# Seven products for eight in one pair of inner units of the FFN's down projection

## The chip, the cores and the metric

The program runs on one core of one Trainium2 chip, in one launch. The metric is the device time of one execution in microseconds (us), lower is better. It is compared as the median of several runs.

## The reference

One inference step of a two-layer streaming encoder for 512 prompt rows and 8 x 16 = 128 sample rows, 640 rows of width 1024 in all, which share the weights. Each layer is a mixer and a gated FFN, both between RMS norms:

```python
def swiglu(x, wg, wu, wd):
    return (jax.nn.silu(x @ wg) * (x @ wu)) @ wd
...
        xp = xp + rms_norm(mp, norm_mix_post[layer])
        fp = swiglu(rms_norm(xp, norm_ffn_pre[layer]), ffn_w_gate[layer], ffn_w_up[layer], ffn_w_down[layer])
        xp = xp + rms_norm(fp, norm_ffn_post[layer])
```

The hidden width is 2816, that is 22 units of 128. Everything is float32. Only the last product, `@ wd` (the down projection, 640 x 2816 by 2816 x 1024), is touched by the change.

## The kernel before

**Precision.** TensorE multiplies operands of type `fp32r`. To keep float32 accuracy each operand is split into a high part, a rounded copy made by ScalarE, and a low part, the rest, made by VectorE (`split`). A product then takes three matmuls: high by high, high by low and low by high.

**Rows.** The 640 rows are five row tiles of 128 (`TT = 5`), the last with the sample rows. For gate and up, the rows are cut into two halves of 320 (`HT`), and each hidden unit is made by the class `Seven`/`GateUp`: the two column blocks (gate and up), two inner halves and two row halves are a 2 x 2 x 2 block product, which is made with seven products for eight (the Winograd form of Strassen's scheme). Each product is 12 matmuls of 320 columns, so a unit takes 84 matmuls.

**Chunks.** `ffn` takes the 22 units in chunks of 4, 4, 4, 4 and 6 (`CHUNKS`). A chunk first makes its units' hidden rows, transposed, in tiles `hid` (128 inner rows by 640 columns, high and low part), and then runs `out_chunk`, the down stretch: for each row tile `t` and each column half `h` of 512, all units of the chunk are summed in one PSUM bank, with the hidden tile as the stationary operand and 512 columns of the unit's down weights as the moving one:

```python
            def products(h, i):
                for a, w in ((0, 0), (0, 1), (1, 0)):
                    mm(pss[h], acts[i][:, a, cols], weight(i, w, h), ...)
```

When the last unit is in, `leave(h)` takes the bank out: in the first chunk ScalarE copies it to the accumulator `acc[t]`, in later ones VectorE adds it there, with raised priority. So a chunk of four has 5 x 2 x 4 x 3 = 120 matmuls of 512 columns and ten reads of banks. In the first chunk of each FFN two units are made directly, without the seven products, before the other two (`Direct`, `PLAIN = 2`). The last chunk also ends the layer (`fin`), and isn't touched.

**Buffers.** Weights land in `raw` buffers (two, each for two units or for the gate and up of one), through SP's queue. `operand` splits them into `q` buffers (five); a gate-up unit takes four `q` (one of them for 512 columns only), a down stretch of four takes four. `hid` has seven buffers, `t2` (hidden work tiles) seven, PSUM eight banks, `t4` nine, five of which are the accumulator.

**Order.** The generators of all tasks are woven in Python by a clock of estimated matmul times (`Weave`); in the FFN's first four chunks the main task is alone but for the start of the first. The tile framework then sets the order of instructions on each engine before the program runs: an instruction goes into its engine's queue when it is ready by the framework's own estimate, and of several ready ones the first in priority, which is the order of the program unless `tc.high_priority()` raises it. On the chip each engine goes through its queue in that order, with semaphore waits.

In the trace every matmul but the transposes has line L170 (`mm`), and every ScalarE and VectorE instruction L102 (the wrapper `Ordered`). Lines L217 and L219 load down weights, L521 and L522 the weights of a gate-up unit. The names are `ps` for a bank, `q` for operands, `hid` for the hidden tiles, `x` for the normed input, `t` for work tiles and the accumulator.

Of the kernel before, what the change touches and what calls it, by code (L numbers as in the profile page):

```python
# [9 lines left out]
F32R = mybir.dt.float32r  # L10
AF = mybir.ActivationFunctionType
ALU = mybir.AluOpType
AX = mybir.AxisListType

P = 128
D = 1024
# [3 lines left out]
NT = NP + NS  # L20
TT = NT // P
# [3 lines left out]
HT = NT // 2  # L25
# [8 lines left out]
PLAIN = 2  # L34
# [6 lines left out]
CACHE = 5200.0  # L41
LAND = 2500.0
DIRECT = ((8, 12),)


class Event:
# [62 lines left out]
def trunk_kernel(  # L109
# [41 lines left out]
    nc = tc.nc  # L151
    act, dve = Ordered(tc, nc.scalar), Ordered(tc, nc.vector)
# [4 lines left out]
    qp = ctx.enter_context(tc.tile_pool(name="qp", bufs=5))  # L157
# [9 lines left out]
    def mm(out, lhsT, rhs, start, stop, n, share=1, more=False):  # L167
        fast = lhsT.dtype == F32R
        W.now += PASS * (max(n, 256) if fast else 4 * n / share) + 2
        nc.tensor.matmul(out, lhsT=lhsT, rhs=rhs, start=start, stop=stop, skip_group_check=more)  # L170
# [7 lines left out]
    def nm(s):  # L178
        uid[0] += 1
        return f"{s}{uid[0]}"  # L180

    def bank(shape=(P, 512)):
        return psp.tile(list(shape), F32, tag="ps", name=nm("ps"))

    def t4(shape):
        return t4p.tile(list(shape), F32, tag="t4", name=nm("t4_"))

    def t2(shape):
        return t2p.tile(list(shape), F32, tag="t2", name=nm("t2_"))
# [19 lines left out]
    def raw():  # L209
        return rawp.tile([P, 5, 512], F32, tag="raw", name=nm("raw"))  # L210

    def fetch(srcs):

        for i, src in enumerate(srcs):
            if i % 2 == 0:
                w = raw()[:, :4, :].rearrange("p (h a) c -> p h (a c)", h=2)
                nc.sync.dma_start(out=w[:, 0, :], in_=src)  # L217
                if i + 1 < len(srcs):
                    nc.sync.dma_start(out=w[:, 1, :], in_=srcs[i + 1])  # L219
            yield w[:, i % 2, :]  # L220

    def operand(src):
        n = src.shape[-1]
        q = qp.tile([P, 2, D], F32R, tag="q", name=nm("q"))
        split((q[:, 0, :n], q[:, 1, :n]), src)
        return q

    def unit(feed):
        return operand(next(feed))

    def split(dst, val):
        act.copy(out=dst[0], in_=val)
        dve.tensor_tensor(out=dst[1], in0=val, in1=dst[0].bitcast(F32), op=ALU.subtract)
# [6 lines left out]
    class Norm:  # L240


        def __init__(self):
            self.ms = None
# [16 lines left out]
    class Normed:  # L261
# [8 lines left out]
        def take(self, t, ps):  # L270
            c = slice(t * P, (t + 1) * P)
            for i in range(2):
                split((self.h[i][:, :, c], self.l[i][:, :, c]), ps[i])
            W.signal(self.ev[t], 1600)
# [161 lines left out]
    def hid_tile():  # L436
        return hidp.tile([P, 2, NT], F32R, tag="hid", name=nm("hid"))

    def out_chunk(acts, srcs, acc, first, last, fin, tail=None):
        feed = fetch(srcs)  # L440
        hls = [unit(feed) for _ in srcs[:5]]
        n = len(acts)
        spare = [[t2([P, 512]).bitcast(F32R) for _ in range(2)] for _ in range(2)] if n > 5 else None
        if spare:
            x = next(feed)
            for h in range(2):
                split(spare[h], x[:, h * 512 : (h + 1) * 512])

        def weight(i, w, h):
            if i < 5:  # L450
                return hls[i][:, w, h * 512 : (h + 1) * 512]
            return spare[h][w]

        for t in range(TT):
            cols = slice(t * P, (t + 1) * P)
            if tail is not None and t == TT - 1:
                yield from tail()
            pss = [bank(), bank()]
            if first:
                acc[t] = t4([P, D])  # L460

            def products(h, i):
                for a, w in ((0, 0), (0, 1), (1, 0)):
                    mm(
                        pss[h],
                        acts[i][:, a, cols],
                        weight(i, w, h),
                        i == 0 and a == 0 and w == 0,
                        i == n - 1 and a == 1,
                        512,  # L470
                    )

            def leave(h):
                o = acc[t][:, h * 512 : (h + 1) * 512]
                if first:
                    act.copy(out=o, in_=pss[h])
                else:
                    with tc.high_priority():
                        dve.tensor_tensor(out=o, in0=pss[h], in1=o, op=ALU.add)
                if last:  # L480
                    fin(t, h, acc[t], pss[h])

            early = n - 1 if t == 0 else EARLY if t == TT - 1 else 0
            for i in range(early):
                for h in range(2):
                    products(h, i)
                yield
            for h in range(2):
                for i in range(early, n):
                    products(h, i)  # L490
                    if i % 2 and i < n - 1:
                        yield
                leave(h)
                yield

    def in_row(t):
        return xp[t * P : (t + 1) * P, :] if t < 4 else xs

# [83 lines left out]
    class GateUp(Seven):  # L582


        def __init__(self, layer, f, X):
            super().__init__(wgate[layer, f], wup[layer, f], X)
            self.one = t2([P, 2, HT])
            self.two = t2([P, 2, HT])
            self.p5 = self.two[:, 1, :]
            self.hid = hid_tile()  # L590
# [12 lines left out]
        def c21(self, a):  # L603
            gate, up = self.two[:, 0, :], self.two[:, 1, :]
            act.activation(out=gate, in_=a, func=AF.Silu)
            dve.tensor_tensor(out=up, in0=up, in1=gate, op=ALU.mult)
            split((self.hid[:, 0, HT:], self.hid[:, 1, HT:]), up)

    class Units(Seven):

# [49 lines left out]
    class Direct(Plain):  # L660
# [4 lines left out]
        def leave(self, col, cols, ps):  # L665
            if col == 0:
                self.t = t2([P, 2, HT])
                act.activation(out=self.t[:, 0, :], in_=ps, func=AF.Silu)
            else:
                t = self.t[:, 1, :]  # L670
                dve.tensor_tensor(out=t, in0=ps, in1=self.t[:, 0, :], op=ALU.mult)
                split((self.hid[:, 0, cols], self.hid[:, 1, cols]), t)
# [16 lines left out]
    def ffn(layer, X, make):  # L689
        hid = {}  # L690
        acc = {}
        f0 = 0
        for c, n in enumerate(CHUNKS):
            fs = list(range(f0, f0 + n))
            rest = fs
            if c == 0:
                rest = fs[PLAIN:]
                lead = [Direct(layer, f, X) for f in fs[:PLAIN]]
                for low in range(2):
                    for i, g in enumerate(lead):  # L700
                        yield from g.rows(low)
                        if (low, i) == (0, PLAIN - 1):
                            ahead = GateUp(layer, rest[0], X)
                            ahead.prepare()
                for f, g in zip(fs, lead):
                    hid[f] = g.hid
            for f in rest:
                g = ahead if f == PLAIN else GateUp(layer, f, X)
                yield from g.steps()
                hid[f] = g.hid  # L710
            last = c == len(CHUNKS) - 1
            yield from out_chunk(
                [hid[f] for f in fs],
                [wdown[layer, f * P : (f + 1) * P, :] for f in fs],
                acc,
                c == 0,
                last,
                make() if last else None,
            )
            f0 += n  # L720
# [5 lines left out]
    def even_mixer(X, hls):  # L726
# [58 lines left out]
        def pairs(todo):  # L785
# [3 lines left out]
            def make():  # L789
                i, j, _ = todo[len(made)]  # L790
                p = (PlainUnits if (i, j) in DIRECT else Units)(ev_t[i], ev_t[j], X)
                p.prepare()
# [99 lines left out]
        def mixed_pair(g):  # L892
# [17 lines left out]
            False,  # L910
            True,
            make_fin(gpost, in_row, x_row, X2),
        )
        return X2
# [368 lines left out]
    def main():  # L1283
# [4 lines left out]
        def load(t):  # L1288
            xt.append(t4([P, D]))
            nc.sync.dma_start(out=xt[t], in_=in_row(t))  # L1290
# [52 lines left out]
        def mid():  # L1343
            gpost = bcast(g_ffn_post[0], D, t4)
            nxt.append(Normed(bcast(g_mix_pre[1], D, t4)))
            return make_fin(gpost, x_row, x_row, nxt[0])

        yield from ffn(0, X, mid)
        X = yield from odd_mixer(nxt[0])

        def end():
            gpost = bcast(g_ffn_post[1], D, t4)
            return make_fin(gpost, x_row, y_row, None)

        yield from ffn(1, X, end)

    W.spawn(main(), 9)
# [95 lines left out]
```

## Time and profile before

| what | value |
|---|---|
| median of 3 runs | 1312.57 us (1312.55 to 1312.61) |
| the profiled execution | 1312.65 us, of which the span is 1310.9 us |
| TensorE busy | 1293.6 us, 99% of the span |
| weight loads (PEld, beside the matmuls) | 1178.0 us, 90% |
| VectorE (DVE) busy | 891.6 us, 68% |
| ScalarE (ACT) busy | 615.3 us, 47% |
| granted TensorE clock | 0.999 of full speed |

A row of a timeline gives the start from the span's begin, the time up to the end of the group, engine, line, operation, what it writes and reads, the shapes, the count, and in brackets the idle time before it and what ended that. A row of the groups ends in the busy time in us, the mean of one instruction in ns, and the idle time before. A row of the stages gives, for a stretch from A to B, its length and the busy time of each engine with the number of instructions in brackets. Matmuls overlap, so the time of one is read from the distance of the starts, not from its mean duration.

### The profile page before, as it was taken

Reading aid. Unit: us, or ns where it says so; the run is one execution under the profiler, and the core shown is the slowest. Engines: PE = TensorE matmul, PEld = TensorE weight load, DVE = VectorE, ACT = ScalarE, POOL = GpSimd, SP = SyncE. Lnnn points to the kernel's source line nnn. Section 1 sums busy time; section 2 is a strip of 40 time slices with the busy share of each in tenths; the row PEclk is TensorE's granted clock in tenths of the full one; section 3 lists DMA queues with packets and bytes.
Section 4 is the critical chain, followed back from the end, with each engine's and each line's share of the span. In section 5 each row is a group of like instructions: output and inputs, shape, how many; then the busy total and the mean of one; then the engine's idle time right before and its main releaser. Section 6 shows DMA issues by size and latency. Waiting matters only on the chain. (4 is left out here: it accounts for less than half of the span.)

```text
span 1310.9 us, 20085 instructions
## 1 busy us (share of the span) xinstructions
PE 1293.6 (99%) x8066; PEld 1178.0 (90%) x8066; DVE 891.6 (68%) x1458; ACT 615.3 (47%) x1134; POOL 54.4 (4%) x107
## 2 busy tenths in 40 slices
PE   8999999999999999999999999999999999999997
PEld 6999988989899998998799886689999898999996
DVE  7986779737576665777646555689567575766765
ACT  6545547535254352554433455466455252534541
POOL 2100110000000000001110000010000000000000
PEclk9999999999999999999999999999999999999999
DMA  7112452211223121245335435732213031221242
GB/s 251 73 65 97 146 177 97 97 63 68 95 80 114 65 97 56 75 148 189 143 120 185 154 139 195 287 130 89 97 64 129 32 116 46 97 97 64 97 140 102
DMA packets 45965, 150.12 MB, mean 115 GB/s; under 512 B 6576, under 2 KB 8496, under 8 KB 45872
## 3 DMA queue, kind: packets, MB, share of 16 engines
q1 hardware_dynamic: 45872, 148.84, 31.3%
q8 instruction: 63, 1.03, 0.3%
q14 instruction: 30, 0.25, 0.1%
HBM read 133.57 MB, written 15.26 MB: 114 GB/s over the span
## 5 line engine op out<-in xcount | busy, mean ns | idle before, releaser
L170 PE MATMUL ps<-x,q 128*128 128x320 f32 (+2 forms) x4884 | 727.5, 310 | 3.0 <-DVE q L102 1.8
L170 PEld LDWEIGHTS ps<-x,q 128*128 128x128 f32 x4884 | 717.6, 188 | 8.0 <-issue 2.9
L170 PE MATMUL ps<-q,hid 128*128 128x512 f32 x1710 | 402.8, 392 | 0.0
L102 ACT CAST q<-raw 128x1024 fp32r<-128x1024 f32 (+1 forms) x276 | 267.4, 976 | 281.3 <-PE ps L170 230.2
L102 DVE TENSOR_TENSOR q<-raw,q 128x1024 fp32r<-128x1024 f32 (+1 forms) x276 | 310.6, 1128 | 129.8 <-ACT q L102 125.0
L170 PEld LDWEIGHTS ps<-q,hid 128*128 128x128 f32 x1710 | 318.2, 188 | 67.2 <-ACT t L102 1.0
L102 ACT COPY t<-ps 128x320 f32<-128x320 f32 (+2 forms) x304 | 135.6, 452 | 198.2 <-PE ps L170 170.0
L102 DVE TENSOR_TENSOR t<-ps,t 128x512 f32<-128x512 f32 (+2 forms) x164 | 100.5, 616 | 92.6 <-PE ps L170 92.4
L102 DVE TENSOR_TENSOR raw<-raw 128x512 f32<-128x512 f32 x141 | 122.0, 866 | 5.0 <-DMA raw<-in_dram 2.8
L102 DVE TENSOR_TENSOR t<-t,t 128x512 f32<-128x512 f32 (+4 forms) x107 | 58.2, 552 | 48.7 <-ACT t L102 46.3
L237 POOL TENSOR_TENSOR st<-st,mhalf 128x1 f32<-128x1 f32 x45 | 30.4, 677 | 992.4 <-DVE st L102 988.4
L102 DVE SCALAR_TENSOR_TENSOR t<-t,st,t 128x512 f32<-128x512 f32 (+1 forms) x61 | 54.2, 916 | 21.2 <-POOL st L237 19.6
L102 ACT ACTIVATE t<-t 128x320 f32<-128x320 f32 (+1 forms) x60 | 40.2, 669 | 42.1 <-issue 22.7
L102 ACT ACTIVATE ps<-t 128x512 f32<-128x512 f32 x40 | 24.1, 604 | 63.3 <-DVE t L102 63.2
L102 ACT CAST hid<-t 128x320 fp32r<-128x320 f32 (+1 forms) x96 | 46.3, 484 | 9.5 <-DVE t L102 7.6
L102 DVE TENSOR_TENSOR t<-t 128x320 f32<-128x320 f32 (+3 forms) x90 | 48.8, 543 | 1.8 <-ACT t L102 0.4
L102 DVE TENSOR_TENSOR hid<-t,hid 128x320 fp32r<-128x320 f32 (+1 forms) x96 | 49.0, 513 | 0.1
L170 PE MATMUL ps<-q,x 128*128 128x512 f32 x192 | 46.5, 395 | 2.3 <-DVE q L102 1.8
L170 PEld LDWEIGHTS ps<-q,x 128*128 128x128 f32 x192 | 35.5, 188 | 11.4 <-DVE q L102 2.9
L102 DVE TENSOR_TENSOR t<-t,ps 128x320 f32<-128x320 f32 x47 | 22.9, 488 | 32.8 <-PE ps L170 32.8
L174 PE MATMUL ps<-ident,t 128*128 128x128 f32 x288 | 40.9, 276 | 3.2 <-DVE t L102 1.9
L174 PEld LDWEIGHTS ps<-ident,t 128*128 128x128 f32 x288 | 32.8, 140 | 11.4 <-issue 6.0
(97 smaller groups left out, 550.3 us busy)
## 6 DMA issues: line engine op xcount, KB each, us to landing
raw<-in_dram SPq DMA_DIRECT2D x184, 512.0 KB, 4.1
x<-in_dram SPq DMA_DIRECT2D x24, 512.0 KB, 6.4
t<-in_dram SPq DMA_DIRECT2D x22, 512.0 KB, 5.5
xbuf<-t SPq DMA_DIRECT2D x15, 512.0 KB, 2.8
t<-xbuf SPq DMA_DIRECT2D x15, 512.0 KB, 3.9
out_dram<-t SPq DMA_DIRECT2D x15, 256.0 KB, 2.0
c<-in_dram SPq DMA_DIRECT2D x4, 512.0 KB, 4.3
fscr<-x SPq DMA_DIRECT2D x2, 768.0 KB, 3.3
```

The source lines that it names most:

```text
L102: ins = op(*args, **kw)
L170: nc.tensor.matmul(out, lhsT=lhsT, rhs=rhs, start=start, stop=stop, skip_group_check=more)
L174: nc.tensor.transpose(out=out, in_=in_, identity=ident)
L237: nc.gpsimd.tensor_tensor(out=r, in0=ms, in1=mhalf, op=ALU.pow)
```

## The change

In each of the first four chunks of each FFN, one pair of inner units is taken out of the plain sums of the down stretch: units 0 and 1 of the chunk, in the first chunk units 2 and 3 (`CROSSED`). For this pair the down product is a 2 x 2 x 2 block product again: the inner halves are the two units, the column halves the two of 512, and the row halves are row tiles 0 and 1 against row tiles 3 and 4 (`FAR = 3`). It is made with seven products for eight. Row tile 2 and the other two units stay as they were, as plain products, which go into the same banks where they can.

- `Sums` makes four combinations of the pair's hidden rows (256 columns each) on VectorE from the unsplit values, in the work tiles that the two units hold, and splits them into two more `hid` buffers.
- `Weights` holds the pair's weights in one `raw` buffer, splits the plain ones into two `q` (`take`), then makes four combinations in place, in two steps of two (`early`: T2 and T1, `late`: T3 and T4), each step splitting into one `q` more.
- `crossed_chunk` stands in the place of `out_chunk`. Partial sums that serve two outputs are read from a bank while its sum goes on: bank `a[t]` is added to the left half of row tile t, then with S2 T2 to the right half, then with S3 T3 to the right half of row tile t + 3, then with the second unit's T4 and the plain units to the left half of row tile t + 3. Bank `c[t]` takes S1 T1 to row tile t + 3 and then S4 and the plain units to row tile t, right half.
- The first unit of a pair splits its lower hidden rows only up to row 384, since row tiles 3 and 4 of it are used in the sums alone (`low`).

```diff
+CROSSED = {0: ((2, 3),), 1: ((0, 1),), 2: ((0, 1),), 3: ((0, 1),)}
+FAR = 3
+Q = 2 * P
...
+    class Sums:
+        def __init__(self, one, two, hold):
+            a11, a21 = one.one[:, 1, :Q], one.two[:, 1, HT - Q :]
+            a12, a22 = two.one[:, 1, :Q], two.two[:, 1, HT - Q :]
+            s1, s2, s3, s4 = (x[:, 0, :Q] for x in (two.two, two.one, one.one, one.two))
+            self.s = [hold[i // 2][:, :, i % 2 * Q : (i % 2 + 1) * Q] for i in range(4)]
+            for i, (out, x, y, op) in enumerate(
+                (
+                    (s1, a21, a22, ALU.add),
+                    (s2, s1, a11, ALU.subtract),
+                    (s3, a11, a21, ALU.subtract),
+                    (s4, a12, s2, ALU.subtract),
+                )
+            ):
+                dve.tensor_tensor(out=out, in0=x, in1=y, op=op)
+                split((self.s[i][:, 0, :], self.s[i][:, 1, :]), out)
+
+    class Weights:
+        def __init__(self, srcs):
+            self.w = w = raw()
+            for i in range(2):
+                nc.sync.dma_start(out=self.both(i), in_=srcs[i])
+            self.q = []
+        def take(self, i):
+            self.q.append(operand(self.both(i)))
...
+        def sub(self, out, x, y):
+            w = self.w
+            dve.tensor_tensor(out=w[:, out, :], in0=w[:, x, :], in1=w[:, y, :], op=ALU.subtract)
+        def halves(self, x):
+            q = qp.tile([P, 2, D], F32R, tag="q", name=nm("q"))
+            q4 = q.rearrange("p x (a c) -> p x a c", a=2)
+            split((q4[:, 0], q4[:, 1]), x)
...
+        def early(self):
+            self.sub(4, 1, 0)
+            self.sub(0, 3, 4)
+            self.t2, self.t1 = self.halves(self.w[:, 0:5:4, :])
+        def late(self):
+            self.sub(1, 3, 1)
+            self.sub(2, 2, 0)
+            self.t3, self.t4 = self.halves(self.w[:, 1:3, :])
+
+    def crossed_chunk(acts, pairs, sums, srcs, acc, first):
+        ws = [Weights([srcs[i] for i in p]) for p in pairs]
+        for w in ws:
+            for i in range(2):
+                w.take(i)
...
+        for i in rest:
+            hls[i] = unit(feed)
+        for w in ws:
+            w.early()
+        for w in ws:
+            w.late()
...
+        def leave(t, h, ps):
+            o = acc[t][:, h * 512 : (h + 1) * 512]
+            if first and (t, h) not in written:
+                written.add((t, h))
+                with tc.high_priority():
+                    act.copy(out=o, in_=ps)
+                return
+            with tc.high_priority():
+                dve.tensor_tensor(out=o, in0=ps, in1=o, op=ALU.add)
...
+        near = range(TT - FAR)
+        a = [bank() for _ in near]
+        for t in near:
+            products(a[t], [(act_rows(p[0], t), wt(p[0], 0)) for p, _, _ in every])
+            leave(t, 0, a[t])
+            yield
+        for t in near:
+            b = bank()
+            products(b, [(act_rows(p[1], t), wt(p[1], 0)) for p, _, _ in every] + plain(t, 0))
+            leave(t, 0, b)
+            yield
+        for t in range(TT - FAR, FAR):
+            for h in range(2):
+                b = bank()
+                products(b, plain(t, h, range(len(acts))))
+                leave(t, h, b)
+                yield
+        c = [bank() for _ in near]
+        for n, (p, w, s) in enumerate(every):
+            begin, end = n == 0, n == len(every) - 1
+            for t in near:
+                products(a[t], [(sum_rows(s, 1, t), w.t2)], False, end)
+                if end:
+                    leave(t, 1, a[t])
+            yield
+            for t in near:
+                products(c[t], [(sum_rows(s, 0, t), w.t1)], begin, end)
+                if end:
+                    leave(t + FAR, 1, c[t])
+            yield
+        for t in near:
+            products(c[t], [(sum_rows(s, 3, t), wt(p[1], 1)) for p, _, s in every] + plain(t, 1), False)
+            leave(t, 1, c[t])
+            yield
+        for t in near:
+            products(a[t], [(sum_rows(s, 2, t), w.t3) for _, w, s in every], False)
+            leave(t + FAR, 1, a[t])
+            yield
+        if rest:
+            for t in near:
+                b = bank()
+                products(b, plain(t + FAR, 1))
+                leave(t + FAR, 1, b)
+                yield
+        for t in near:
+            products(a[t], [(act_rows(p[1], t + FAR), w.t4) for p, w, _ in every] + plain(t + FAR, 0), False)
+            leave(t + FAR, 0, a[t])
+            yield
...
     class GateUp(Seven):
-            split((self.hid[:, 0, HT:], self.hid[:, 1, HT:]), up)
+            split((self.hid[:, 0, HT : self.low], self.hid[:, 1, HT : self.low]), up[:, : self.low - HT])
...
     def ffn(layer, X, make):
-                g = ahead if f == PLAIN else GateUp(layer, f, X)
+                g = ahead if f == PLAIN else GateUp(layer, f, X, P * FAR if f - f0 in summed else NT)
                 yield from g.steps()
                 hid[f] = g.hid
+                made[f - f0] = g
+                for m, p in enumerate(crossed):
+                    if p[1] == f - f0:
...
+                        sums.append(Sums(*(made[i] for i in p), hold))
             last = c == len(CHUNKS) - 1
+            if crossed:
+                yield from crossed_chunk(
...
+                f0 += n
+                continue
             yield from out_chunk(
```

More of the change, by code (lines that the diff above doesn't have):

```diff
@@ new lines, in trunk_kernel, with both @@
+    class Weights:
[6 more added lines that the diff above has]
+            self.q.append(operand(self.both(i)))
+        def both(self, i):
+            return self.w[:, 2 * i : 2 * i + 2, :].rearrange("p a c -> p (a c)")
+        def sub(self, out, x, y):
[5 more added lines that the diff above has]
+            split((q4[:, 0], q4[:, 1]), x)
+            return ([q[:, x, a * 512 : (a + 1) * 512] for x in range(2)] for a in range(2))
+        def early(self):
[6 more added lines that the diff above has]
+            self.t3, self.t4 = self.halves(self.w[:, 1:3, :])
@@ new lines, in crossed_chunk, with wt, act_rows, sum_rows @@
+    def crossed_chunk(acts, pairs, sums, srcs, acc, first):
[3 more added lines that the diff above has]
+                w.take(i)
+        hls = {i: q for p, w in zip(pairs, ws) for i, q in zip(p, w.q)}
+        rest = [i for i in range(len(acts)) if i not in hls]
+        feed = fetch([srcs[i] for i in rest])
+        for i in rest:
[4 more added lines that the diff above has]
+            w.late()
+        every = list(zip(pairs, ws, sums))
+        written = set()
+        def wt(i, h):
+            return [hls[i][:, x, h * 512 : (h + 1) * 512] for x in range(2)]
+        def act_rows(i, t):
+            return [acts[i][:, x, t * P : (t + 1) * P] for x in range(2)]
+        def sum_rows(s, i, t):
+            return [s.s[i][:, x, t * P : (t + 1) * P] for x in range(2)]
+        def products(ps, parts, start=True, stop=True):
+            last = 3 * len(parts) - 1
+            for n, (a, b) in enumerate(parts):
+                for i, (x, y) in enumerate(((0, 0), (0, 1), (1, 0))):
+                    mm(
+                        ps,
+                        a[x],
+                        b[y],
+                        start and n + i == 0,
+                        stop and 3 * n + i == last,
+                        512,
+                        more=not (start and stop),
+                    )
+        def plain(t, h, units=rest):
+            return [(act_rows(i, t), wt(i, h)) for i in units]
+        def leave(t, h, ps):
[7 more added lines that the diff above has]
+                dve.tensor_tensor(out=o, in0=ps, in1=o, op=ALU.add)
+        if first:
+            for t in range(TT):
+                acc[t] = t4([P, D])
+        near = range(TT - FAR)
[46 more added lines that the diff above has]
+            yield
@@ L582, in trunk_kernel, with __init__ @@
     class GateUp(Seven):
-        def __init__(self, layer, f, X):
+        def __init__(self, layer, f, X, low=NT):
             super().__init__(wgate[layer, f], wup[layer, f], X)
+            self.low = low
             self.one = t2([P, 2, HT])
@@ L702, in ffn @@
                         if (low, i) == (0, PLAIN - 1):
-                            ahead = GateUp(layer, rest[0], X)
+                            ahead = GateUp(layer, rest[0], X, P * FAR if CROSSED.get(c) else NT)
                             ahead.prepare()
@@ L706, in ffn @@
                     hid[f] = g.hid
+            crossed = CROSSED.get(c, ())
+            summed = [p[0] for p in crossed]
+            made, sums = {}, []
             for f in rest:
-                g = ahead if f == PLAIN else GateUp(layer, f, X)
+                g = ahead if f == PLAIN else GateUp(layer, f, X, P * FAR if f - f0 in summed else NT)
                 yield from g.steps()
                 hid[f] = g.hid
-            last = c == len(CHUNKS) - 1
+                made[f - f0] = g
+                for m, p in enumerate(crossed):
+                    if p[1] == f - f0:
+                        hold = [
+                            t4([P, 2, 2 * Q]).bitcast(F32R) if m else hid_tile()[:, :, : 2 * Q] for _ in range(2)
+                        ]
+                        sums.append(Sums(*(made[i] for i in p), hold))
+            last = c == len(CHUNKS) - 1
+            if crossed:
+                yield from crossed_chunk(
+                    [hid[f] for f in fs],
+                    crossed,
+                    sums,
+                    [wdown[layer, f * P : (f + 1) * P, :] for f in fs],
+                    acc,
+                    c == 0,
+                )
+                f0 += n
+                continue
             yield from out_chunk(
```

## The prediction

> **What bounds the kernel now.** I read the busy shares first, then TensorE's own timeline, then the busy times stage by stage, then the groups of instructions by shape, and last the places where TensorE waited.
>
> ```profile
> span 1310.9 us, 20085 instructions
> ## 1 busy us (share of the span) xinstructions
> PE 1293.6 (99%) x8066; PEld 1178.0 (90%) x8066; DVE 891.6 (68%) x1458; ACT 615.3 (47%) x1134; POOL 54.4 (4%) x107
> ...
> PEclk9999999999999999999999999999999999999999
> ```
>
> TensorE is busy for 1293.6 of 1310.9 us at the full clock, so 17.3 us of idle time is all that anything other than fewer or shorter matmuls could win. VectorE at 68% is the next. The span and what lies around it make 1312.65 us for the profiled execution, 0.08 us above the median of the runs shown (1312.57); I make the sum against 1312.65 and take 0.08 off.
>
> ```profile
> 288.77 49.44 PE L170 MATMUL ps<-x,q 128*128 128x320 f32 x336
> 338.04 27.39 PE L170 MATMUL ps<-q,hid 128*128 128x512 f32 x120
> 365.27 49.44 PE L170 MATMUL ps<-x,q 128*128 128x320 f32 x336
> ```
>
> This is the second chunk of the first FFN: four gate-up units, 336 matmuls, then the down stretch, 120 matmuls. No idle time stands between the rows, so starts tell the pitch: (365.27 - 338.04) / 120 = 226.9 ns for a matmul of 512 columns, and (338.04 - 288.77) / 336 = 146.6 ns for one of 320.
>
> ```profile
> core 0: us, PE busy (x) PEld busy (x) DVE busy (x) ACT busy (x) POOL busy (x), PEclk, DMA share, GB/s
> 42.00:73.00 31.00, 31.00 (x220) 30.88 (x220) 28.48 (x49) 16.18 (x26) 5.08 (x11) 1.00 0.28 104
> 261.50:288.80 27.30, 27.30 (x123) 22.60 (x122) 7.42 (x11) 9.28 (x16) 0.00 (x0) 1.00 0.11 39
> 288.80:338.00 49.20, 49.20 (x337) 49.20 (x336) 36.62 (x51) 28.09 (x47) 0.00 (x0) 1.00 0.30 107
> 338.00:365.30 27.30, 27.30 (x123) 22.60 (x122) 13.37 (x20) 3.98 (x7) 0.00 (x0) 1.00 0.10 39
> ```
>
> In the down stretch (338.00 to 365.30) VectorE works 13.37 of 27.3 us and ScalarE 3.98; in the gate-up stretch before it 36.62 and 28.09 of 49.2. TensorE alone sets the time there. The first row matters too: with VectorE busy for 28.48 of 31.0 us (92%) TensorE still lost nothing.
>
> **What the change removes.** In a down stretch each row tile and column half takes 4 units x 3 matmuls, 5 x 2 x 12 = 120. Counted from the new function: 6 (first unit of the pair, row tiles 0 and 1, left half), 18 (second unit and the two plain ones there), 24 (row tile 2, both halves, all four units), 6, 6, 18, 6 (the products with T2, T1, S4 and T3), 12 and 18 (the plain units and T4 on row tiles 3 and 4): 114. All have 512 columns and the same 128x128 stationary tile. So 6 x 226.9 ns = 1.361 us go from each of eight stretches (four in each of two FFNs): **10.9 us**. This count also excludes that the change removes no work.
>
> [...]
>
> **What the change adds off TensorE.** The rows for one instruction of each kind:
>
> ```profile
> L102 DVE TENSOR_TENSOR q<-raw,q 128x1024 fp32r<-128x1024 f32 x227 | 277.0, 1224 | 87.2 <-ACT q L102 82.4
> L102 ACT CAST q<-raw 128x1024 fp32r<-128x1024 f32 x227 | 236.9, 1052 | 107.1 <-PE ps L170 62.4 <-issue 17.7 <-DVE t L102 12.6
> L102 DVE TENSOR_TENSOR t<-ps,t 128x512 f32<-128x512 f32 x106 | 72.5, 689 | 86.7 <-PE ps L170 86.6
> L102 DVE TENSOR_TENSOR raw<-raw 128x512 f32<-128x512 f32 x94 | 64.7, 688 | 4.6 <-DMA raw<-in_dram 2.8
> L102 DVE TENSOR_TENSOR hid<-t,hid 128x320 fp32r<-128x320 f32 x88 | 42.7, 486 | 0.1
> L102 DVE TENSOR_TENSOR x<-t,x 128x256 fp32r<-128x256 f32 x12 | 4.4, 420 | 0.3 <-ACT x L102 0.3
> L102 ACT CAST x<-t 128x256 fp32r<-128x256 f32 x12 | 4.1, 400 | 0.0
> L102 DVE TENSOR_TENSOR t<-t,f 128x256 f32<-128x256 f32 x6 | 2.6, 428 | 0.0
> L102 DVE TENSOR_TENSOR hid<-x,hid 128x128 fp32r<-128x128 f32 x4 | 1.0, 283 | 0.0
> ```
>
> - Four activation sums of 256 columns and their splits: VectorE 4 x 0.43 + 4 x 0.42 = 3.4 us, ScalarE 4 x 0.40 = 1.6 us.
> - Four weight differences of 512 columns, 4 x 0.69 = 2.8 us, and two splits of 1024, 2 x 1.22 = 2.4 us on VectorE and 2 x 1.05 = 2.1 us on ScalarE.
> - Partial sums leave the banks 18 times instead of 10: 8 x 0.69 = 5.5 us more on VectorE (in the first chunk the ten first writes stay on ScalarE, as now).
> - The first unit's lower hidden split shrinks from 320 to 64 columns: 0.2 to 0.3 us less.
>
> Together 13.8 us more VectorE and 3.5 us more ScalarE in a chunk. VectorE's 13.37 us in the down stretch become about 13.4 + 10.4 = 23.8 of 25.9 us (92%), the same share as in the stretch at 42 to 73 us, where TensorE lost nothing. In chunks 2 to 4 the sums fall into the third gate-up unit: VectorE has 49.20 - 36.62 = 12.6 us free in four units, 3.1 in one, against 3.4; the fourth unit takes the rest, and the sums aren't wanted before 48 matmuls (10.9 us) into the down stretch. In the first chunk the pair is the last two units, so its sums stand at the start of the down stretch; there VectorE has only 7.42 us to do, and the sums, the first weight pair and the unit's own rest (3.4 + 2.6 + some 2 us, four operations near 0.49) fit the 10.9 us. I cost all this at nothing. Without that cover the price is the part that overhangs: up to 2 us a chunk if VectorE runs that far behind.
>
> **Buffers and loads.** The transfers stay two times two 512 KB on SP's queue; the pair's raw buffer is held until T3 and T4 are split.
>
> ```profile
> 314.22 0.33 SPq L217 DMA_DIRECT2D raw<-in_dram  x1
> ...
> 331.82 0.33 SPq L521 DMA_DIRECT2D raw<-in_dram  x1
> ...
> 339.14 0.33 SPq L521 DMA_DIRECT2D raw<-in_dram  x1
> ```
>
> ```profile
> 361.43 0.62 ACT L102 CAST q<-raw 128x512 fp32r<-128x512 f32 x1 [21.02 <-PE ps L170]
> ```
>
> ```profile
> raw<-in_dram SPq DMA_DIRECT2D x184, 512.0 KB, 4.1
> ```
>
> (SP's timeline, ScalarE's, and the page's list of transfers with the time to landing.) The first down weights are asked for at 314.2, now and after, and land 4.1 us later, some 20 us before the stretch. The next two units' weights are now asked for at 331.8 and 339.1. After the change the first goes out when the plain pair's buffer is split (about 339) and the second when T3/T4 are split. T3/T4 need the operand buffer of the pair's first unit, free after 48 matmuls at 338.04 + 10.9 = 348.9, so cast (1.05) and split (1.22) end near 351.5. The second load lands 4.1 us later, some 8 us before the new end of the stretch (338.04 + 114 x 0.2269 = 363.9), and its unit comes a unit later still. Nothing else in these stretches is queued behind it on SP. T3 itself is wanted after 78 matmuls, 6.8 us after its buffer is free, 4.5 us more than it needs. The next unit's operands, which now wait for a buffer until 361.43, get T1/T2's buffer after 60 matmuls (351.7) and the second unit's after 72 (354.4). All hidden; if VectorE lagged by more than 4.5 us, T3 would be late next.
>
> One need moves forward: in the first chunk the last unit's hidden rows are wanted after 6 matmuls instead of 18.
>
> ```profile
> 261.54 27.39 PE L170 MATMUL ps<-q,hid 128*128 128x512 f32 x120
> ```
>
> ```profile
> 261.51 0.46 ACT L102 CAST hid<-t 128x320 fp32r<-128x320 f32 x1 [0.43 <-DVE t L102]
> ```
>
> ```profile
> 262.53 0.49 DVE L102 TENSOR_TENSOR hid<-t,hid 128x320 fp32r<-128x320 f32 x1
> ```
>
> Their high part is done at 261.97 and wanted at 261.54 + 1.36 = 262.90, the low part at 263.02 and wanted two matmuls later, 263.35. It is covered, by 0.3 us; if the sums came in between, up to 1 us in two of the eight stretches would be lost.
>
> **The one wait that I price.** One bank is filled with T1 products (row tile 3), read by VectorE, and then added to again by S4 products (row tile 0), with only row tile 4's three T1 matmuls between: 3 x 226.9 = 0.68 us.
>
> ```profile
> 343.23 1.28 DVE L102 TENSOR_TENSOR t<-ps,t 128x512 f32<-128x512 f32 x2
> ...
> 349.15 0.69 DVE L102 TENSOR_TENSOR t<-ps,t 128x512 f32<-128x512 f32 x1 [2.03 <-PE ps L170]
> ```
>
> The fourth group of 12 ends at 338.04 + 48 x 0.2269 = 348.93; its read starts at 349.15, 0.22 us after, and lasts 0.69. So the bank is free 0.91 us after its last matmul, and TensorE is ready after 0.68: 0.23 us are lost, and a return signal for which no row stands alone. From below the wait is zero, if other matmuls are put there; from above it is 0.23 + 1.22 = 1.45 us, if a split of 1024 has just begun. The trace shows that the planner does put other work there:
>
> ```profile
> 221.33 1.92 PE L170 MATMUL ps<-a,q 128*128 128x320 f32 x12
> 223.09 0.31 PE L170 MATMUL ps<-x,q 128*128 128x320 f32 x1
> 223.24 0.60 PE L170 MATMUL ps<-a,q 128*128 128x320 f32 x3
> 225.07 1.88 PE L170 MATMUL ps<-x,q 128*128 128x320 f32 x11 [1.23 <-DVE x L102]
> ```
>
> After one matmul of the second half three of the next column were drawn forward, though too few: 1.23 us were lost. I take 0.3 us a stretch, near the unfilled turn with VectorE free, since 0.68 us per three matmuls against four reads at 0.64 us each (1.28 for two) leaves it just in step. 8 x 0.3 = 2.4 us.
>
> **Sum.** 1312.65 - 10.9 + 2.4 = 1304.2, less 0.08: **1304.1 us**, 0.65% faster. Its own range, for 0.1 to 0.6 us lost in a stretch, is 1302.5 to 1306.5.
>
> **Rivals.**
> - *Everything hidden.* The planner fills the bank turn from the twelve plain matmuls on row tiles 3 and 4, which need only a free bank. 1312.65 - 10.9 - 0.08 = 1301.7. For it: the drawn-forward rows, and the idle-free stretch at 92%. Against it: the 1.23 us in those same rows.
> - *VectorE late where the planner thought it in time.* One wait as in the row at 225.07, 1.23 us, in every stretch: 1312.65 - 10.9 + 9.8 - 0.08 = 1311.5, no change; in half of them, 1306.6 and still faster. For it: 92% busy in the down stretch and the turn's thin cover. Against it: the same share at 42 to 73 us cost nothing.
> - *Slower: T3/T4's preparation stands ahead of the reads.* Place: VectorE's queue between the T2 products and the S4 products. If both differences (2 x 0.69) and the split (1.22) stand before the read of that bank, and the matmuls behind are in fixed order, the turn costs 0.3 + 2.6 = 2.9 us: 1312.65 - 10.9 + 23.2 - 0.08 = 1324.9. It decides from 1.36 us a stretch on. Against it: the differences need only landed weights, which are there some 20 us before the stretch, and the reads have raised priority. [...]
>
> **Chances.** Forecast 0.52, everything hidden 0.22, partly lost but faster 0.11, no change 0.07, slower 0.08. Faster by over 0.2% (2.6 us, about what a measurement here can tell from no change) 0.85, within it 0.07, slower 0.08. The range 1301.2 to 1310.5 leaves out the last two cases and little more; the count bounds it below.
>
> **What would show it.** The eight rows of 120 matmuls become 114 and shorten from 27.23 to about 25.9 us of pitch; any idle of TensorE stands in front of the S4 products, released by VectorE's read into the accumulator; VectorE's busy time grows by about 8 x 13.8 = 110 us and ScalarE's by 28; gate-up stretches stay at 49.27. It is wrong if the matmul pitch rises above 226.9 ns, if gate-up stretches grow (sums or loads late), or if idle of over 1.4 us stands in most down stretches.

## The result

The changed kernel takes 1301.91 us (median of 4 runs, 1301.86 to 1301.96) against 1312.59 us (4 runs, 1312.55 to 1312.66): ratio 0.9919, 95% interval 0.9901 to 0.9936, 10.7 us faster. The forecast was 1304.1 with a range of 1301.2 to 1310.5; the time is the one that the rival "everything hidden" gave, 1301.7, and lies 0.7 us above the lower end of the range.

The busy shares of the changed kernel:

```profile
span 1300.2 us, 20234 instructions
## 1 busy us (share of the span) xinstructions
PE 1284.1 (99%) x8018; PEld 1169.1 (90%) x8018; DVE 985.9 (76%) x1634; ACT 641.1 (49%) x1182; POOL 54.2 (4%) x107
```

48 matmuls are gone (8066 to 8018), VectorE has 94.3 us more to do (891.6 to 985.9) and ScalarE 25.8 us more (615.3 to 641.1).

### The profile page after: what moved, and what is told of

Its sections match the earlier page's. It is cut to its first block, busy times and chain, and to the rows that moved or that the text cites. A ratio compares the mean times of both kernels' runs of the same rounds, so it can differ in the third digit from the quotient of the medians.

```text
span 1300.2 us, 20234 instructions
## 1 busy us (share of the span) xinstructions
PE 1284.1 (99%) x8018; PEld 1169.1 (90%) x8018; DVE 985.9 (76%) x1634; ACT 641.1 (49%) x1182; POOL 54.2 (4%) x107
## 5 line engine op out<-in xcount | busy, mean ns | idle before, releaser
L105 ACT CAST q<-raw 128x1024 fp32r<-128x1024 f32 (+1 forms) x292 | 283.8, 978 | 256.1 <-PE ps L173 185.9
L105 DVE TENSOR_TENSOR q<-raw,q 128x1024 fp32r<-128x1024 f32 (+1 forms) x292 | 329.7, 1132 | 91.8 <-ACT q L105 85.9
L173 PE MATMUL ps<-q,hid 128*128 128x512 f32 x1662 | 392.3, 392 | 0.0
L173 PEld LDWEIGHTS ps<-q,hid 128*128 128x128 f32 x1662 | 309.1, 188 | 65.8 <-ACT t L105 1.3
L105 DVE TENSOR_TENSOR t<-ps,t 128x512 f32<-128x512 f32 (+2 forms) x228 | 140.8, 632 | 37.2 <-PE ps L173 36.8
L105 DVE TENSOR_TENSOR raw<-raw 128x512 f32<-128x512 f32 (+1 forms) x173 | 142.6, 831 | 5.3 <-DMA raw<-in_dram 3.1
L105 DVE TENSOR_TENSOR t<-t,t 128x320 f32<-128x320 f32 (+4 forms) x131 | 68.2, 528 | 40.0 <-ACT t L105 36.8
L105 ACT CAST hid<-t 128x320 fp32r<-128x320 f32 (+3 forms) x128 | 56.5, 451 | 15.9 <-DVE t L105 14.3
L105 DVE TENSOR_TENSOR hid<-t,hid 128x320 fp32r<-128x320 f32 (+3 forms) x128 | 59.2, 470 | 0.1
L105 DVE TENSOR_TENSOR t<-t 128x320 f32<-128x320 f32 (+4 forms) x98 | 52.1, 531 | 1.6
```

The source lines that it names most:

```text
L105: ins = op(*args, **kw)
```

## The profile after

TensorE's timeline of the changed kernel, first and second chunk of the first FFN (start, length, what it runs, count):

```profile
261.55 26.13 PE L173 MATMUL ps<-q,hid 128*128 128x512 f32 x114
287.52 49.44 PE L173 MATMUL ps<-x,q 128*128 128x320 f32 x336
336.80 26.05 PE L173 MATMUL ps<-q,hid 128*128 128x512 f32 x114
362.68 49.44 PE L173 MATMUL ps<-x,q 128*128 128x320 f32 x336
```

The down stretch of the second chunk goes from 27.23 us to 362.68 - 336.80 = 25.88; 114 x 0.2269 is 25.87. In the first chunk it is 287.52 - 261.55 = 25.97, 0.10 more than its matmuls. The gate-up stretch keeps 336.80 - 287.52 = 49.28 us. No idle time stands in brackets in these rows.

The busy times of the same two stages (length, then PE, PEld, DVE, ACT, POOL with counts, granted clock, DMA share, GB/s):

```profile
287.50:336.80 49.30, 49.30 (x338) 49.27 (x336) 41.30 (x62) 29.90 (x52) 0.00 (x0) 1.00 0.24 86
336.80:362.70 25.90, 25.90 (x117) 21.41 (x116) 20.59 (x31) 5.70 (x8) 0.00 (x0) 1.00 0.22 82
```

VectorE now works 20.59 of 25.9 us in the down stretch (13.37 of 27.3 before) and 41.30 of 49.3 in the gate-up stretch (36.62 before). The new work is split between the two.

VectorE's timeline around the turn of the T1 banks in the second chunk, and ScalarE's cast of T3 and T4:

```profile
347.00 1.23 DVE L105 TENSOR_TENSOR q<-raw,q 128x1024 fp32r<-128x1024 f32 x1 [1.12 <-ACT q L105]
348.14 3.17 DVE L105 TENSOR_TENSOR t<-ps,t 128x512 f32<-128x512 f32 x5
351.71 1.23 DVE L105 TENSOR_TENSOR q<-raw,q 128x1024 fp32r<-128x1024 f32 x1 [0.40 <-ACT q L105]
```

```profile
345.92 1.05 ACT L105 CAST q<-raw 128x1024 fp32r<-128x1024 f32 x1 [5.83 <-PE ps L173]
```

Five reads of banks run without a break: the last of row tile 2, two behind T2, two behind T1. The prediction had counted four of them. T3 and T4 are split at 348.23, 2.2 us before the T1 products end (336.80 + 60 x 0.2269 = 350.41). What the planner made of that is in the program's order on TensorE, which is no view of the profile (bank, operands, count; `hid_3103` and `hid_3104` hold the sums, `q_3385` T2 and T1, `q_3390` T3 and T4, `q_3371` the second unit's weights, the second chunk; only the part from T2 to the first S4 product is shown):

```
MATMUL ps_3393<-q_3385,hid_3103 x3      S2 T2
MATMUL ps_3394<-q_3385,hid_3103 x3
MATMUL ps_3453<-q_3385,hid_3103 x3      S1 T1
MATMUL ps_3454<-q_3385,hid_3103 x3
MATMUL ps_3393<-q_3390,hid_3104 x2      S3 T3, drawn forward
MATMUL ps_3453<-q_3371,hid_3104 x3      S4, the same bank as S1 T1
```

Two T3 matmuls stand in the turn in chunks 2 to 4, one in the first chunk.

## The experiments

**Fixed order.** Is there a wait in the turn at all?

```diff
+        ins = nc.tensor.matmul(...)
+        if fixed[0]:                      # only in products() of crossed_chunk
+            tc.keep_in_program_order(ins)
```

> The changed kernel with the matmuls of the crossed down stretches pinned in the order in which they are written, so that no later matmul can be drawn into the turn of a bank. Theory A (there is a wait of 0.23 us and a signal between VectorE's read of the T1 bank and the S4 products, and the changed kernel hides it under T3 matmuls drawn forward): 0.25 to 0.5 us idle in front of S4 in each of eight stretches, 1303.9 to 1305.9 us, near 1304.3. Rival B (the read is in time anyway, and the order gives nothing): 1301.9 us, no idle.

Measured: 1304.74 us (before, on the same chip, 1312.71; ratio 0.9939, 0.9922 to 0.9955). TensorE's timeline:

```profile
261.70 26.36 PE L174 MATMUL ps<-q,hid 128*128 128x512 f32 x114
287.90 49.44 PE L174 MATMUL ps<-x,q 128*128 128x320 f32 x336
337.17 26.43 PE L174 MATMUL ps<-q,hid 128*128 128x512 f32 x114
363.44 49.44 PE L174 MATMUL ps<-x,q 128*128 128x320 f32 x336
```

The stretch of the second chunk takes 363.44 - 337.17 = 26.27 us, 0.40 more than its 114 matmuls; the first, where ScalarE reads the T1 banks, 26.20, 0.33 more. Six times 0.40 and twice 0.33 are 3.1 us; the changed kernel loses 0.3 us itself (below), and this one is 2.8 us over it. Theory A holds, B falls. Single rows around the turn of the second chunk show where the 0.40 us go (the first is VectorE's reads of the two T1 banks; PEld is the weight load):

```profile
350.32 1.37 DVE L105 TENSOR_TENSOR t<-ps,t 128x512 f32<-128x512 f32 x2
351.06 0.30 PEld L174 LDWEIGHTS ps<-q,hid 128*128 128x128 f32 x2 [0.53 <-DVE t L105]
351.06 0.50 PE L174 MATMUL ps<-q,hid 128*128 128x512 f32 x1
351.40 0.39 PE L174 MATMUL ps<-q,hid 128*128 128x512 f32 x1
```

The last T1 matmul's slot ends at 337.17 + 60 x 0.2269 = 350.78, and the first S4 matmul starts at 351.06, 0.28 us late. The next one starts 0.34 us after it instead of 0.227, which is the other 0.11: the weight load of the first S4 matmul waited for the same read and starts with it. No row shows an idle time of TensorE in brackets here: a matmul's record lasts some 0.39 us while the next starts after 0.227, so 0.16 us of such a gap is covered by the modelled end and the rest is small: it must be read from the distance of the starts.

**Turn filled by hand.** Is that turn all that a fixed order costs?

```diff
             for t in near:
                 products(c[t], [(sum_rows(s, 0, t), w.t1)], begin, end)
...
+        if rest:
+            for t in near: ... products(b, plain(t + FAR, 1)); leave(t + FAR, 1, b)
         for t in near:
             products(c[t], [(sum_rows(s, 3, t), wt(p[1], 1)) ... ] + plain(t, 1), False)
```

(The block is taken away from its old place; the matmuls are pinned as above.)

> Matmuls pinned in written order as in the run with fixed order, but the twelve plain matmuls on row tiles 3 and 4, right half, are written between the T1 and the S4 products: 2.72 us of other work in the bank's turn instead of none. Theory (all of the loss with fixed order is this one turn, 0.40 us where VectorE reads and 0.33 us where ScalarE reads): the loss goes whole, 1301.6 us, 0.3 us under the changed kernel, whose drawn-forward matmuls leave about 0.1 us in the first chunk and 0.02 us in the others. Rival (fixed order loses time elsewhere too): 1302.5 to 1304.5 us.

> The changed kernel once more, beside the three others on the same chip, as their base: 1301.9 us, 0.9919 of the kernel before.

Measured: 1301.98 us (1301.78 to 1302.30), beside 1302.00 (1301.76 to 1302.56) for the changed kernel on the same chip. TensorE's timeline (first, second and fourth chunk):

```profile
261.65 21.95 PE L174 MATMUL ps<-q,hid 128*128 128x512 f32 x96
283.44 1.04 PE L174 MATMUL ps<-x,q 128*128 128x320 f32 x6
284.32 4.27 PE L174 MATMUL ps<-q,hid 128*128 128x512 f32 x18
288.43 48.56 PE L174 MATMUL ps<-x,q 128*128 128x320 f32 x330
336.82 21.95 PE L174 MATMUL ps<-q,hid 128*128 128x512 f32 x96
...
487.14 21.95 PE L174 MATMUL ps<-q,hid 128*128 128x512 f32 x96
```

The 2.8 us of the fixed order are gone whole, so it was this one turn. The further 0.3 us can't be told in the times, whose spread was larger here. From the first chunk's down stretch to the fourth's it was 487.14 - 261.65 = 225.49 us in the one trace and 487.27 - 261.69 = 225.58 in the other, 0.09 us less. Nearly all of that is the first chunk: 288.43 - 261.65 - 6 x 0.1466 = 25.90 us against 287.66 - 261.69 = 25.97. The 0.02 us of the other chunks stay with a filled turn, so they aren't a wait in it. The moved block leaves another turn open, that of the banks between T3 and T4. There the planner put matmuls of the next gate-up unit, which aren't pinned: the six in the second row, four in the later chunks.

**Side work alone.** Does the added work on VectorE and ScalarE cost anything by itself?

```diff
-        near = range(TT - FAR)
-        ...                                # the seven products
+        for t in range(TT):
+            for h in range(2):
+                b = bank()
+                products(b, plain(t, h, range(len(acts))))
+                leave(t, h, b)
+                yield
```

> Only the side work of the change: the activation sums, the weight differences and all the splits are made and held as in the changed kernel, but the down stretches run all eight products (120 matmuls) and read ten banks; nothing reads the sums. Theory A (the side work is hidden behind TensorE): 1312.6 us, within 0.3. Rival B (VectorE or the longer held buffers cost something): above 1313.0 us, with idle of TensorE in or after the down stretches.

Measured: 1312.62 us against 1312.71, ratio 0.9999 (0.9990 to 1.0008). Its page and the stages of its second chunk:

```profile
PE 1294.1 (99%) x8066; PEld 1177.9 (90%) x8066; DVE 950.8 (73%) x1570; ACT 642.9 (49%) x1182; POOL 54.3 (4%) x107
```

```profile
288.90:338.10 49.20, 49.20 (x337) 49.19 (x336) 41.26 (x62) 29.87 (x52) 0.00 (x0) 1.00 0.24 86
338.20:365.40 27.20, 27.20 (x121) 22.51 (x121) 15.95 (x23) 5.72 (x8) 0.00 (x0) 1.00 0.21 78
```

VectorE does 59.2 us more than before (7.4 a chunk), and TensorE isn't later by anything that can be measured. Theory A. This is 59.2 of the 94.3 us that the change adds: the eight more reads of banks a stretch aren't in it, and the first unit's lower rows are split whole here (the edit takes `low` out too).

**Products alone.** The other half: the same matmuls and reads without sums and combinations.

```diff
-        for w in ws:
-            w.early()
-        for w in ws:
-            w.late()
...
+        def sum_rows(p, i, t):
+            return act_rows(p[0], t)
+        for p, w in zip(pairs, ws):
+            w.t1 = w.t2 = w.t3 = wt(p[0], 1)
+            w.t4 = wt(p[1], 0)
```

> Only the seven products: the same 114 matmuls, banks and eighteen reads in the order of the change, but without the activation sums and without the weight combinations; plain hidden rows and plain weights stand in their place, so the pair's share of the output is not the down product. Theory A (the saving is 48 matmuls of 226.9 ns and the side work costs nothing): 1301.6 to 1302.0 us, as the changed kernel. Rival B (the side work costs part of the saving): below 1301.4 us.

Measured: 1303.01 us (1302.85 to 1303.21), neither theory: it is slower than the kernel that does more.

```profile
336.68 26.20 PE L173 MATMUL ps<-q,hid 128*128 128x512 f32 x114
362.72 49.44 PE L173 MATMUL ps<-x,q 128*128 128x320 f32 x336
```

A stretch takes 362.72 - 336.68 = 26.04 us, 0.17 over its matmuls. In this program's order one matmul is drawn into the turn in every chunk, where the changed kernel has two in chunks 2 to 4. That fits the turn within 0.04 us: 0.40 unfilled, less 0.227 for one matmul leaves 0.17 (0.21 was lost in the third chunk), less two leaves nothing; and where ScalarE reads, 0.33 - 0.227 = 0.10, as in the changed kernel's first chunk (0.06 in this run's). Why the planner drew only one here was not tried; that it thought VectorE's read earlier, with less on VectorE, is only argued.

**Preparation ahead of the reads.** The slower rival, built on purpose, first with fixed matmuls, then with free ones:

```diff
-        for w in ws:
-            w.late()
...
+            Ordered.on = True
+            w.late()                       # behind the T2 products, ahead of the reads of the T1 banks
             for t in near:
                 products(c[t], [(sum_rows(s, 0, t), w.t1)], begin, end)
                 if end:
                     leave(t + FAR, 1, c[t])
+            Ordered.on = False
```

> The slower rival built on purpose: the differences, the cast and the split for T3 and T4 are traced behind the T2 products and pinned on VectorE and ScalarE ahead of the reads of the T1 banks, and the matmuls are pinned in written order. By the rival's own price, 2.9 us a stretch: near 1325 us. If the cast, which must stand between the differences and the split, comes in series too (1.05 us more) and the turn itself costs 0.35 to 0.40 us: about 4 us a stretch in chunks 2 to 4 and 2.8 us in the first, where ScalarE reads the T1 bank: 1330 to 1334 us. If VectorE's queue order does not matter: 1304.7 us, as with the fixed matmul order alone.

> The same preparation pinned ahead of the reads, but the matmuls in the order that the planner chooses. Theory (the planner covers a turn that it foresees, with the twelve plain matmuls of row tiles 3 and 4, 2.72 us, and the T3 products behind them, 1.36 us): 1301.9 to 1304 us. Rival (the drawn-forward work covers only small turns): half of the loss stays, 1310 us and more.

Measured with fixed matmuls: 1341.92 us, ratio 1.0223 (1.0208 to 1.0238), above both sums (1325, and 1330 to 1334). TensorE's timeline (the first row is of the first chunk, the others of the second) and VectorE's at the turn of the second:

```profile
276.20 12.55 PE L174 MATMUL ps<-q,hid 128*128 128x512 f32 x54 [0.75 <-ACT t L105]
...
337.86 13.79 PE L174 MATMUL ps<-q,hid 128*128 128x512 f32 x60
355.29 14.00 PE L174 MATMUL ps<-q,hid 128*128 128x512 f32 x54 [3.64 <-DVE t L105]
369.13 49.44 PE L174 MATMUL ps<-x,q 128*128 128x320 f32 x336
```

```profile
350.94 1.28 DVE L105 TENSOR_TENSOR raw<-raw 128x512 f32<-128x512 f32 x2
353.41 1.23 DVE L105 TENSOR_TENSOR q<-raw,q 128x1024 fp32r<-128x1024 f32 x1 [1.19 <-ACT q L105]
354.55 1.28 DVE L105 TENSOR_TENSOR t<-ps,t 128x512 f32<-128x512 f32 x2
```

The differences, 1.19 us of waiting for ScalarE's cast, and the split stand before the first read, which starts at 354.55, though its bank was there for it from 337.86 + 57 x 0.2269 + 0.22 = 351.01 on. The starts tell 355.29 - (337.86 + 60 x 0.2269) = 3.82 us of delay where the rival had priced 2.9: it had left out the cast in series. In the first chunk the wait reads 0.75 us and the stretch grew by 1.0, where I had expected 2.8: there VectorE has made the differences by 270.99 already, and only the cast, 1.05 us from 274.61 on, stands ahead of ScalarE's two reads at 275.56. Nearly all the rest of the excess in chunks 2 to 4 is the clock: in the second the 54 matmuls after the wait took 369.13 - 355.29 = 13.84 us where 54 x 0.2269 is 12.25. The granted clock (the column before the last two) before and after the wait of the second chunk:

```profile
350.00:355.00 5.00, 1.65 (x8) 1.03 (x6) 3.81 (x6) 1.99 (x2) 0.00 (x0) 1.00 0.00 0
355.00:360.00 5.00, 4.71 (x14) 3.79 (x15) 4.06 (x6) 0.19 (x1) 0.00 (x0) 0.66 0.58 210
360.00:365.00 5.00, 5.00 (x23) 4.14 (x23) 4.19 (x7) 0.43 (x1) 0.00 (x0) 1.00 0.00 0
```

Measured with free matmuls: 1304.08 us, 2.1 over the changed kernel beside it, the upper end of the theory's range. TensorE's timeline:

```profile
336.89 24.30 PE L173 MATMUL ps<-q,hid 128*128 128x512 f32 x105
361.03 0.60 PE L173 MATMUL ps<-x,q 128*128 128x320 f32 x3
361.46 2.22 PE L173 MATMUL ps<-q,hid 128*128 128x512 f32 x9
363.52 49.00 PE L173 MATMUL ps<-x,q 128*128 128x320 f32 x333
412.35 24.29 PE L173 MATMUL ps<-q,hid 128*128 128x512 f32 x105
```

A chunk takes 412.35 - 336.89 = 75.46 us against 75.16 in the changed kernel (412.10 - 336.94 in the trace beside it), 0.30 more, where the fixed order lost 5.4 (31.27 instead of 25.88 in the stretch). In the program's order all twelve plain matmuls and five of the six with T3 stand in the turn in chunks 2 to 4 (17 x 0.2269 = 3.86 us), two plain ones and two with T3 in the first chunk, and three matmuls of the next unit come near the end of the stretch. What is still lost in chunks 2 to 4 stands in front of the first T3 matmul and right behind it, 0.13 and 0.11 us by the starts, and no longer in front of S4.

**Two pairs.** How much more can VectorE take, and is there a faster version?

```diff
-CROSSED = {0: ((2, 3),), 1: ((0, 1),), 2: ((0, 1),), 3: ((0, 1),)}
+CROSSED = {0: ((2, 3),), 1: ((0, 1), (2, 3)), 2: ((0, 1), (2, 3)), 3: ((0, 1), (2, 3))}
```

> The changed kernel with both pairs of units in chunks 2 to 4 (units 0 and 1, and units 2 and 3), the first chunk as it is. Six more matmuls fall away in each of six stretches, 8.2 us. Theory A (TensorE stays the only bound): 1293.8 us. Theory B (VectorE becomes the bound: its 41.3 + 20.5 us of 75.2 grow by some 8 us, and the second pair's sums now stand at the start of the down stretch; eight operand buffers are wanted where five exist): part of it is lost, 1295 to 1301 us, with idle of TensorE in front of the products with T2 or T3. Above 1301.9 us if the operands of the next unit come late too.

Measured: 1294.16 us (1294.01 to 1294.51), ratio 0.9859 to the kernel before (0.9844 to 0.9873): faster than both kernels. Stages of its third chunk and the frame of its second down stretch:

```profile
361.70:411.00 49.30, 49.30 (x337) 49.26 (x336) 45.30 (x71) 29.83 (x52) 0.00 (x0) 1.00 0.25 86
411.00:435.50 24.50, 24.50 (x110) 20.21 (x109) 21.85 (x36) 8.20 (x12) 0.00 (x0) 1.00 0.24 86
```

```profile
337.20 13.79 PE L173 MATMUL ps<-q,hid 128*128 128x512 f32 x60
...
361.73 49.44 PE L173 MATMUL ps<-x,q 128*128 128x320 f32 x336
```

108 matmuls in 361.73 - 337.20 = 24.53 us, 108 x 0.2269 = 24.51. VectorE is busy for 45.30 of 49.3 us (92%) in the gate-up stretch and 21.85 of 24.5 (89%) in the down stretch, and TensorE loses nothing. Theory A; B falls, in its operand buffers too. The 0.4 us over 1293.8 stand ahead of these stretches: the first down stretch starts at 261.99 here and at 261.55 in the changed kernel.

## Why the prediction was right, and where it was off

**The removed matmuls** were right: 114 for 120, at an unchanged pitch (25.88 / 114 = 227.0 ns), 10.9 us. The side-work run (the same time within 0.1 us) and the unchanged gate-up stretches show that the added work neither costs nor gives anything.

**The priced wait is the term that failed**: "I take 0.3 us a stretch, near the unfilled turn with VectorE free", 2.4 us in all. The mechanism and nearly the size were right for an unfilled turn: 0.40 us with VectorE, 0.33 with ScalarE. It was wrong to price the turn unfilled. In the changed kernel the stretches take 0.10 us more than their matmuls in the two first chunks and some 0.02 in the six others, 0.3 us in all, and 1312.65 - 10.9 + 0.3 - 0.08 = 1302.0 meets the measured 1301.91. The rows that I had quoted for drawn-forward work pointed to the other choice, though 1.23 us were lost in them. So the case that I gave 0.52 did not come about, and the one that I gave 0.22 did. The forecast's direction rests on the count; that its number is only 2.2 us off comes from the small price, not from a right view of the turn.

**What fills it** was also wrong in the details. I named only the plain matmuls as cover. I had T3 and T4 ready at 348.9 + 1.05 + 1.22 = 351.2 (written as "near 351.5"), hardly ahead of the end of the T1 products at 338.04 + 60 x 0.2269 = 351.65, because I let the pair's first operand buffer go only after 48 matmuls. In row tile 2 of chunks 2 to 4 the first unit comes first, so its last use is the 39th, and ScalarE's cast starts at 345.92, right behind that (336.80 + 39 x 0.2269 = 345.65). So T3 products, not the plain ones, stand in the turn.

**The missing signal**, which I had no row for: reading takes 0.22 + 0.69 us and three matmuls cover 0.68, so of the 0.40 us measured 0.17 are left. By the rows of the fixed order only some 0.05 of that is the way back (the first read ends at 350.32 + 0.69 = 351.01, the first S4 matmul starts at 351.06); the other 0.11 is the late start of the second S4 matmul. That this comes from the weight load, which started only with the matmul (both at 351.06, after 0.53 us without a load), is read from its row and was not tried by itself.

**VectorE's load** was set too high. I had 13.8 us a chunk and 92% of the down stretch; 94.3 / 8 = 11.8 us and 20.59 of 25.9 (79%) were measured. Reads that follow each other take 0.63 us (3.17 for five), not 0.69, and part of the weight differences and splits went into the gate-up stretch, which grew by 4.7 us where I had 3.4. It didn't matter: two pairs run at 89% and 92% for free, and no stretch of the changed kernel has a wait of 1.23 us, which settles the rival "VectorE late".

**Buffers and loads** came as worked out. SP's timeline after:

```profile
337.62 0.33 SPq L685 DMA_DIRECT2D raw<-in_dram  x1
...
348.25 0.33 SPq L685 DMA_DIRECT2D raw<-in_dram  x1
```

The prediction, moved to the new start of the stretch (1.24 us earlier), had some 337.8 and 350.3; the second is sooner because T3 and T4 are.

**The slower rival** was a real mechanism, too cheaply priced and not present. With the preparation pinned ahead and the matmuls fixed it costs 40 us and makes the kernel slower than before; some 25 us of that are the waits (six of 3.82 us and two of 1 us), near the 23.2 priced, and nearly all the rest is the clock (mean granted 0.986, and 0.998 in the changed kernel beside it). That a read keeps its place in VectorE's queue the prediction took as given; in that run it did: both reads stand behind the split, at 354.55, where the bank of the first was there from 351.01. What kept the rival away is that the planner put the preparation earlier and, where that is forbidden, drew other matmuls into the turn: 2.1 us instead of 40.

## What to carry to other kernels

Where TensorE is the only bound, count matmuls first: the saving is their number times the pitch read from the starts, and added work on another engine can cost nothing, as it did here with VectorE busy for 92% and 89% of two stages in a row (two pairs). Price a read that stands between two sums in one bank by its full turn, here 1.08 us (the 0.68 us that three matmuls cover and the 0.40 us lost with the order fixed), and look for as many independent matmuls as that takes before you charge it. If an order is pinned, put that work into the turn by hand, and see which other turn it covered before.

## What was not expected of the hardware

A gap of 3.8 us cost more than itself. In the run with the preparation ahead the granted clock fell to half behind each gap in chunks 2 to 4, for 3.4 us in the second chunk and for 6.8 us in the fourth (in the third its mean was 0.70 from 435 to 440 us and 0.96 from 440 to 445):

```profile
355.05:358.47 3.42, 3.18 (x8) 2.51 (x9) 3.14 (x4) 0.00 (x0) 0.00 (x0) 0.50 0.82 292
515.48:522.30 6.82, 5.77 (x14) 4.57 (x15) 5.24 (x7) 0.33 (x2) 0.00 (x0) 0.50 0.41 154
```

The 54 matmuls behind the gap took 1.6 us more than at full clock in the second chunk and 2.8 us in the fourth (531.61 - 516.53 = 15.08). The 0.75 us wait in the first chunk left the granted clock at 1.00 (276 to 281 us), and so did the 0.28 us in the turn of the fixed order (350 to 355 us) and the 1.22 us wait at 225 us of the changed kernel (222 to 228 us). The third chunk lost 449.83 - 435.83 - 12.25 = 1.8 us, like the second. For the second FFN an estimate from the times has to do: of the 1341.92 - 1302.00 = 39.9 us, 24.9 are waits and 1.6 + 1.8 + 2.8 the loss in the first FFN, which leaves 8.8 us for three stretches, 2.9 each, like the fourth chunk. What decides between the two lengths, and what length of gap is needed, stays open here.
